# A matmul with scale and add on one core: three engines put into loops, transfers sharing semaphores, two tiles per finish

## The chip, the core and the metric

The kernel runs on one core of a Trainium2 chip. The metric is the device time of one execution in microseconds (us), less being better. The core has five engines that run programs of their own: TensorE (PE in the profile, its weight loads PEld), VectorE (DVE), ScalarE (ACT), GpSimd (POOL) and SyncE (SP). They meet at semaphores. The core's 16 DMA engines move data between memory (HBM) and the core's SBUF.

## What is computed

```python
batch, m, k, n = 16, 512, 1024, 768
def reference(x, weight, scale, add_value):
    return (scale * np.matmul(x, weight) + add_value).astype(np.float32)
```

All inputs and the output are float32: x has 16 x 512 rows of 1,024, the weight is 1,024 x 768, scale is 0.1, and add_value and the output have 16 x 512 rows of 768. That is 33.6 MB of x, 3.1 MB of weight, 25.2 MB to add and 25.2 MB to store, 87.0 MB in all.

## The kernel before

The 8,192 rows are taken as 64 tiles of 128 rows. Tiles are grouped by eight: tile s of a group is every eighth row, so that a transfer of eight tiles has one contiguous piece per partition. Each tile passes five steps:

1. SyncE issues its load of x into `xs` (16 slots of one tile) and its load of add_value into `ao` (32 slots).
2. The movers, ScalarE and GpSimd, run the same function `mover` (line 131 issues the copies). Each casts its half of x to bfloat16 into one of two buffers `va`, moving blocks of 32 partitions: eight copies per engine for a block of two or four tiles.
3. VectorE transposes two tiles at a time from `va` to `xt` (four tiles; `turn`, line 154).
4. TensorE multiplies: per tile eight chunks of the 1,024, each against 512 and 256 columns of the weight, into one of four PSUM buffers `mm` (line 194). Its program is a loop over four tiles, 16 turns.
5. VectorE computes scale times product plus add_value into the tile's slot of `ao` (`finish`, line 166), and SyncE stores it from there (line 108).

The weight lands in `ao` slots first and VectorE casts it to bfloat16 (line 142).

SyncE issues every transfer, in the order of the list `STREAM`, written by hand; its entries are (what, first tile, number of tiles), with "w" the weight, "a" add_value and "o" the store. In front of some it waits: for the moves that free the slots of x (lines 92 and 93), for the store that frees a slot of `ao` (line 103), for the finishes that a store needs (line 107). Each of the 29 transfers has a semaphore of its own, `landed`. A wait that isn't met holds all entries behind it.

The order on VectorE is written by hand too: after the finishes of a pair of tiles comes the transpose of the pair after next. The transpose of a block's first pair waits for both movers, and a finish for the landing of its add_value and for the product. ScalarE, GpSimd and VectorE have their programs written out in full, 160 copies each for the first two.

Of the kernel before, what the change touches and what calls it, by code (L numbers as in the profile page):

```python
# [7 lines left out]
P = 128  # L8
G = 8
X_SLOTS = 16  # L10
A_SLOTS = 32
CUT = 512
MM_BUFS = 4
XT_PAIRS = 2
VA_BUFS = 2

STREAM = [
# [5 lines left out]
]  # L23

MOVES = [(t, 2) for t in range(0, 8, 2)] + [(t, 4) for t in range(8, 56, 4)] + [
    (t, 2) for t in range(56, 64, 2)]


@with_exitstack
def kernel(  # L30
# [8 lines left out]
    nc = tc.nc  # L39
    bf16 = mybir.dt.bfloat16  # L40
    fp32 = mybir.dt.float32
# [25 lines left out]
    va = [const.tile([P, 4 * KC, 4, 64], bf16, name=f"va{i}") for i in range(VA_BUFS)]  # L67
    xt = const.tile([P, 2 * XT_PAIRS, KC, P], fp32, name="xt")
    mm = [psum.tile([P, 1024], fp32, name=f"mm{i}") for i in range(MM_BUFS)]

    landed = {key: tc.alloc_semaphore(f"dma{i}") for i, key in enumerate(STREAM)}
    by_act, by_pool, turned, casts, done, made = (
        tc.alloc_semaphore(name)
        for name in ("by_act", "by_pool", "turned", "casts", "done", "made"))

    def transfer(op, t):
        return next(k for k in STREAM if k[0] == op and k[1] <= t < k[1] + k[2])

    def moves_until(t):
        return 8 * sum(1 for s, _ in MOVES if s <= t)  # L80

    def sync_engine(eng):
        for key in STREAM:
            op, s, n = key
            last = s + n - 1
            if op == "w":
                k = A_SLOTS - KJ + s
                dst = ao[:, k:k + n, :].rearrange("p (c r) n -> p c (r n)", r=2)
                move = eng.dma_start(dst, w_v[:, s // 2:(s + n) // 2, :])  # L89
            elif op == "x":  # L90
                if last >= X_SLOTS:
# [3 lines left out]
                move = eng.dma_start(xs[:, k:k + n, :], rows(x_v, s, n))  # L95
            elif op == "a":
                k = s % A_SLOTS
# [6 lines left out]
                move = eng.dma_start(ao[:, k:k + n, :], rows(add_v, s, n))  # L104
            else:
                k = s % A_SLOTS
                eng.wait_ge(made, MM_BUFS + last + 1)
                move = eng.dma_start(rows(out_v, s, n), ao[:, k:k + n, :])
            move.then_inc(landed[key], 16)
        for key in STREAM:  # L110
            if key[0] == "o" and key[1] + key[2] > T - A_SLOTS:
                eng.wait_ge(landed[key], 16)

    def mover(eng, copy, parity, count):
        seen = set()
        used = [None] * VA_BUFS
        turned_after = {}
        for n, (t, size) in enumerate(MOVES):
            buf = n % VA_BUFS
            key = transfer("x", t + size - 1)  # L120
            if key not in seen:
                eng.wait_ge(landed[key], 16)
                seen.add(key)
            if used[buf] is not None:
                eng.wait_ge(turned, used[buf] + size_of[used[buf]])
            used[buf] = t
            k = t % X_SLOTS
            src = xs[:, k:k + size, :].rearrange("p i (c b k) -> p (i c) b k", b=4, k=64)
            for a in (parity, parity + 2):
                for b in range(4):  # L130
                    copy(va[buf][32 * b:32 * b + 32, 0:size * KC, a, :],  # L131
                         src[32 * a:32 * a + 32, :, b, :]).then_inc(count, 1)

    size_of = dict(MOVES)

    def vector_engine(eng):
        seen = set()

        def cast_w(s, n):
            eng.wait_ge(landed["w", s, n], 16)  # L140
            for j in range(s, s + n):
                eng.tensor_copy(w_bf[:, j, :], ao[:, A_SLOTS - KJ + j, :]).then_inc(casts, 1)  # L142

        def turn(t):
            n = next(i for i, (s, size) in enumerate(MOVES) if s <= t < s + size)
            s, size = MOVES[n]
            if t == s:
                eng.wait_ge(by_act, 8 * (n + 1))
                eng.wait_ge(by_pool, 8 * (n + 1))  # L149
            if t >= 2 * XT_PAIRS:  # L150
                eng.wait_ge(done, t - 2 * XT_PAIRS + 2)  # L151
            q = (t - s) * KC
            k = t % (2 * XT_PAIRS)
            eng.transpose(  # L154
                xt[:, k:k + 2, :, :].rearrange("p i c m -> p (i c m)"),
                va[n % VA_BUFS][:, q:q + 2 * KC, :, :].bitcast(fp32).rearrange("p c a k -> p (c a k)"),
            ).then_inc(turned, 2)

        def finish(t):
            key = transfer("a", t)  # L160
            if key not in seen:
                eng.wait_ge(landed[key], 16)
                seen.add(key)
            eng.wait_ge(done, t + 1)
            a = ao[:, t % A_SLOTS, :]
            eng.scalar_tensor_tensor(  # L166
                a, mm[t % MM_BUFS][:, 0:N], float(scale), a,
                op0=mybir.AluOpType.mult, op1=mybir.AluOpType.add).then_inc(made, 1)

        eng.sem_inc(made, MM_BUFS)  # L170
        cast_w(0, 4)
        turn(0)
        cast_w(4, 4)
        turn(2)
        for t in range(T):
            finish(t)
            if t % 2 and t + 3 < T:
                turn(t + 3)

    def tensor_engine(eng):  # L180
        eng.wait_ge(casts, 4)
        with eng.Fori(1, T + 1, 4) as i:
            for q in range(4):
                t = q
                if q % 2 == 0:
                    eng.wait_ge(turned, i + (q + 1))
                for j in range(KJ):
                    if q == 0 and j == 4:
                        eng.wait_ge(casts, KJ)
                    if j == 0:  # L190
                        eng.wait_ge(made, i + q if q else i)
                    x2 = xt[:, q, j // 2, :].bitcast(bf16).rearrange("p (m r) -> p r m", r=2)
                    for n0, n1 in ((0, CUT), (CUT, N)):
                        m = eng.matmul(  # L194
                            mm[q][:, n0:n1], x2[:, j % 2, :], w_bf[:, j, n0:n1],
                            start=(j == 0), stop=(j == KJ - 1))
                m.then_inc(done, 1)

    with tc.tile_critical(no_gpsimd_drain=True):  # L199
        sync_engine(nc.sync)  # L200
        mover(nc.scalar, nc.scalar.copy, 0, by_act)
        mover(nc.gpsimd, nc.gpsimd.tensor_copy, 1, by_pool)
        vector_engine(nc.vector)
        tensor_engine(nc.tensor)

# [34 lines left out]
```

## Time and profile before

| | |
|---|---|
| median of three runs | 211.14 us (210.84 to 212.0) |
| the profiled execution | 211.75 us, of which 210.0 us span |
| mean granted TensorE clock | 0.963 |
| busy: PE, DVE, ACT, POOL | 82%, 49%, 67%, 66% of the span |
| data moved | 87.06 MB, mean 415 GB/s over the span |
| a copy of a mover for four tiles (ACT, POOL) | 1.04 us, 1.03 us; eight in a block |
| a transpose of two tiles (DVE) | 1.24 us |
| a finish of one tile (DVE) | 0.95 us |
| 63 matmuls, about four tiles (PE) | 10.35 us |

The span is the time from the first to the last instruction of the profiled execution; the rest of its time lies outside. Times within the profile are counted from the start of the span. An engine's name with a q (SPq) is its sequencer, which issues transfers and waits. A row of the timeline gives start, duration, engine, line, operation, what is written and read, the number of instructions, and in brackets the engine's idle time before it and what ended it.

### The profile page before, as it was taken

The page shows a single profiled execution, that of the slowest core. Times are in us where ns is not written, and L with a number is a line of the kernel's source. Part 1 is how long each engine was busy: PE and PEld are TensorE (multiplying, and loading weights), DVE is VectorE, ACT ScalarE, POOL GpSimd, SP SyncE. Part 2 cuts the span into 40 slices and gives each one's busy share as a digit, 9 for nine tenths or more (in the row PEclk, how much of TensorE's full clock was granted, in tenths as well). Part 3 has the DMA queues.
Part 4 walks back from the last instruction along what each step waited for, and adds up shares of the span by engine and source line. Part 5 has one row for each costly group of instructions (what it writes and reads, how often), then busy time and mean ns, then how long its engine had stood idle before and what let it go on. Part 6 is the DMA issues. An engine that isn't in the chain of part 4 may idle for free.

```text
span 210.0 us, 2723 instructions
## 1 busy us (share of the span) xinstructions
PE 172.3 (82%) x1008; PEld 101.7 (48%) x1024; DVE 103.2 (49%) x104; ACT 140.8 (67%) x161; POOL 139.5 (66%) x164
## 2 busy tenths in 40 slices
PE   0035949928999999999999999999939999999910
PEld 0012625604655666665566665566615566665500
DVE  0158066116655565556555652766136555447410
ACT  2873980799999896944997069950999249994000
POOL 0884980799999996944998069950999239995000
PEclk9999997996999999999999999999997999999995
DMA  6999899999999999998999999999999999999991
GB/s 215 430 445 449 384 474 399 449 449 399 459 431 412 415 449 418 429 468 375 445 463 415 426 417 421 440 474 395 440 417 446 404 440 445 426 417 421 424 380 76
DMA packets 4435, 87.06 MB, mean 415 GB/s; under 512 B 464, under 2 KB 464, under 8 KB 976
## 3 DMA queue, kind: packets, MB, share of 16 engines
q1 hardware_dynamic: 4432, 87.03, 97.2%
q14 instruction: 3, 0.02, 0.0%
HBM read 61.87 MB, written 25.17 MB: 414 GB/s over the span
## 4 chain that ended last, share of the span: by engine, by line
DMA 43%; POOL 28%; PE 21%; issue 2%; SPq 1%; DVE 1%; DVEq 0%
DMA xs<-in_x_dram 43%; POOL va L131 28%; PE mm L194 21%; SPq L95 1%; DVE xt L154 1%; SPq L89 0%; DVE ao L166 0%; SPq L104 0%; DVEq L151 0%; SPq L93 0%; SPq L235 0%; DVEq L149 0%; SPq L199 0%
## 5 line engine op out<-in xcount | busy, mean ns | idle before, releaser
L194 PE MATMUL mm<-w_bf,xt 128*128 128x256 bf16 (+1 forms) x1008 | 172.3, 332 | 28.1 <-DVE xt L154 24.7
L131 POOL CAST va<-xs 32x1024 bf16<-32x1024 f32 (+1 forms) x160 | 139.3, 870 | 52.7 <-DMA xs<-in_x_dram 42.0
L131 ACT CAST va<-xs 32x1024 bf16<-32x1024 f32 (+1 forms) x160 | 139.5, 872 | 49.8 <-DMA xs<-in_x_dram 43.5
L194 PEld LDWEIGHTS mm<-w_bf,xt 128*128 128x128 bf16 x1024 | 101.7, 100 | 98.4 <-DVE xt L154 25.8
L166 DVE SCALAR_TENSOR_TENSOR ao<-mm,ao 128x768 f32<-128x768 f32 x64 | 60.3, 951 | 65.2 <-PE mm L194 52.3
L154 DVE STREAM_TRANSPOSE xt<-va 128x1024 f32<-128x1024 f32 x32 | 39.5, 1235 | 21.2 <-POOL va L131 19.9
L142 DVE CAST w_bf<-ao 128x768 bf16<-128x768 f32 x8 | 6.0, 804 | 11.8 <-DMA ao<-in_weight_dram 11.8
L131 ACT ACT_TABLE_LOAD x1 | 1.3, 1283 | 0.9 <-SPq L199 0.9
L221 POOL MEMSET const-float32-0.0<- 128x1 f32 x1 | 0.1, 97 | 0.2 <-issue 0.2
L221 POOL MEMSET const-bfloat16-1.0<- 128x1 bf16 x1 | 0.1, 100 | 0.0
L221 POOL MEMSET const-float32-1.0<- 128x1 f32 x1 | 0.1, 98 | 0.0
L221 POOL MEMSET const-uint8-127<- 128x1 uint8 x1 | 0.1, 98 | 0.0
## 6 DMA issues: line engine op xcount, KB each, us to landing
xs<-in_x_dram SPq DMA_DIRECT2D x7, 4096.0 KB, 30.4
ao<-in_add_value_dram SPq DMA_DIRECT2D x8, 3072.0 KB, 31.3
out_dram<-ao SPq DMA_DIRECT2D x7, 3072.0 KB, 35.1
ao<-in_weight_dram SPq DMA_DIRECT2D x2, 1536.0 KB, 10.8
xs<-in_x_dram SPq DMA_DIRECT2D x2, 1024.0 KB, 7.5
xs<-in_x_dram SPq DMA_DIRECT2D x1, 2048.0 KB, 17.7
out_dram<-ao SPq DMA_DIRECT2D x1, 1920.0 KB, 11.0
out_dram<-ao SPq DMA_DIRECT2D x1, 1152.0 KB, 7.0
```

The lines of the kernel that those rows point to most:

```text
L95: move = eng.dma_start(xs[:, k:k + n, :], rows(x_v, s, n))
L131: copy(va[buf][32 * b:32 * b + 32, 0:size * KC, a, :], src[32 * a:32 * a + 32, :, b, :]).then_inc(count, 1)
L142: eng.tensor_copy(w_bf[:, j, :], ao[:, A_SLOTS - KJ + j, :]).then_inc(casts, 1)
L154: eng.transpose(xt[:, k:k + 2, :, :].rearrange("p i c m -> p (i c m)"), va[n % VA_BUFS][:, q:q + 2 * KC, :, :].bitcast(fp32).rearrange("p ...
L166: eng.scalar_tensor_tensor(a, mm[t % MM_BUFS][:, 0:N], float(scale), a, op0=mybir.AluOpType.mult, op1=mybir.AluOpType.add).then_inc(made, 1)
L194: m = eng.matmul(mm[q][:, n0:n1], x2[:, j % 2, :], w_bf[:, j, n0:n1], start=(j == 0), stop=(j == KJ - 1))
L221: nc = _bacc.Bacc("TRN2", target_bir_lowering=False, num_devices=1)
```

## The change

It does these things:

- **Loops.** `mover` becomes a loop of 16 tiles a turn for ScalarE and GpSimd, with four blocks of four tiles in it (the first and last tiles went in blocks of two). VectorE's finishes and transposes become a loop of eight tiles a turn (`group`), the last eight tiles written out behind it; the slot of `ao` is computed from the loop's register. TensorE's loop keeps its four tiles.
- **Shared semaphores.** In place of one for each transfer there are three for x, two for the weight, one for all loads of add_value, two for the stores in turn. A load of add_value now waits until the one before has landed, and a store until the store before the last has. Loads of x wait for the transposes (`turned`) in place of the moves, all but that of tiles 24 to 31.
- **Two tiles per finish.** `mm` becomes one tile with four parts, and one instruction finishes two tiles. TensorE signals and waits once for two tiles. The weight is cast by two instructions in place of eight.
- **The stream.** The first four tiles of x are one transfer (two and two before), the store of tiles 24 to 31 stands behind the loads of add_value 48 to 55 and of x 56 to 63, the last two stores have six and two tiles (five and three before). Slots of `ao` are shifted by eight, so that the weight lies in the first.

```diff
 STREAM = [
-    ("x", 0, 2), ("w", 0, 4), ("x", 2, 2), ("w", 4, 4), ("x", 4, 4), ("a", 0, 8),
+    ("x", 0, 4), ("w", 0, 4), ("w", 4, 4), ("x", 4, 4), ("a", 0, 8),
     ("x", 8, 8), ("a", 8, 8), ("x", 16, 8), ("a", 16, 8), ("x", 24, 8),
     ("a", 24, 8), ("o", 0, 8), ("x", 32, 8), ("o", 8, 8), ("a", 32, 8), ("x", 40, 8),
-    ("o", 16, 8), ("a", 40, 8), ("x", 48, 8), ("o", 24, 8), ("a", 48, 8), ("x", 56, 8),
-    ("o", 32, 8), ("a", 56, 8), ("o", 40, 8), ("o", 48, 8), ("o", 56, 5), ("o", 61, 3),
+    ("o", 16, 8), ("a", 40, 8), ("x", 48, 8), ("a", 48, 8), ("x", 56, 8), ("o", 24, 8),
+    ("o", 32, 8), ("a", 56, 8), ("o", 40, 8), ("o", 48, 8), ("o", 56, 6), ("o", 62, 2),
 ]
...
+    TURNED = MOVE * VA_BUFS
+    MADE = TURNED + 2 + MM_BUFS - 2
+
+    def slot(t):
+        return (t + G) % A_SLOTS
...
                 if last >= X_SLOTS:
-                    eng.wait_ge(by_act, moves_until(last - X_SLOTS))
-                    eng.wait_ge(by_pool, moves_until(last - X_SLOTS))
-                k = s % X_SLOTS
+                    free = last + 1 - X_SLOTS
+                    if s == 24:
+                        eng.wait_ge(by_act, 8 * free // MOVE)
+                        eng.wait_ge(by_pool, 8 * free // MOVE)
+                    else:
+                        eng.wait_ge(turned, TURNED + free)
...
-                if s < A_SLOTS <= last + KJ:
+                if loads:
+                    eng.wait_ge(a_sem, 16 * len(loads))
+                if slot(s) == 0:
                     eng.wait_ge(casts, KJ)
                 if s >= A_SLOTS:
-                    for key2 in STREAM:
-                        if key2[0] == "o" and key2[1] < last + 1 - A_SLOTS and key2[1] + key2[2] > s - A_SLOTS:
-                            eng.wait_ge(landed[key2], 16)
+                    i = stores.index((s - A_SLOTS, n))
+                    eng.wait_ge(o_sem[i % 2], 16 * (i // 2 + 1))
...
-                eng.wait_ge(made, MM_BUFS + last + 1)
+                i = len(stores)
+                if i > 1:
+                    eng.wait_ge(o_sem[i % 2], 16 * (i // 2))
+                eng.wait_ge(made, MADE + last + 1)
...
+    def mover(eng, copy, parity, count, go=None):
+        with eng.Fori(16, 16 * (T // X_SLOTS) + 1, 16) as i:
+            for q in range(X_SLOTS // MOVE):
+                if q < 3:
+                    eng.wait_ge((x_lo, x_mid, x_hi)[q], i)
+                eng.wait_ge(turned, i + (4 * q - 12) if q < 3 else i)
...
+        def finish(pair, at, products):
+            eng.wait_ge(done, products)
+            a = ao_g[:, at, 2 * pair:2 * pair + 2, :]
+            q = 2 * (pair % 2)
             eng.scalar_tensor_tensor(
-                a, mm[t % MM_BUFS][:, 0:N], float(scale), a,
-                op0=mybir.AluOpType.mult, op1=mybir.AluOpType.add).then_inc(made, 1)
+                a, mm[:, q:q + 2, 0:N], float(scale), a,
+                op0=mybir.AluOpType.mult, op1=mybir.AluOpType.add).then_inc(made, 2)
+
+        def group(i, at, last):
+            eng.wait_ge(a_sem, i)
+            for p in range(4):
+                finish(p, at, i + (4 * p - 12) if p < 3 else i)
+                if p < 2 or not last:
+                    turn(1 if p < 2 else 0, p % 2, i + 8 if p == 2 else i)
...
+        with eng.Fori(16, 2 * T, 16) as i:
+            group(i, bass.ds((i // 16) % (A_SLOTS // G), 1), False)
+        s = slot(T - G) // G
+        group(2 * T, slice(s, s + 1), True)
```

In the changed kernel the movers' copies stand on line 137, the casts of the weight on 145, the transposes on 152, the finishes on 161 and the matmuls on 193; SyncE's loads of x are on 100, of add_value on 110, the stores on 118.

More of the change, by code (lines that the diff above doesn't have):

```diff
@@ L13 @@
 MM_BUFS = 4
-XT_PAIRS = 2
+XT_TILES = 4
 VA_BUFS = 2
+MOVE = 4
+AHEAD = 4
 STREAM = [
[1 row of a table removed]
[1 row of a table added]
     ("x", 8, 8), ("a", 8, 8), ("x", 16, 8), ("a", 16, 8), ("x", 24, 8),
     ("a", 24, 8), ("o", 0, 8), ("x", 32, 8), ("o", 8, 8), ("a", 32, 8), ("x", 40, 8),
[2 rows of a table removed]
-]
-MOVES = [(t, 2) for t in range(0, 8, 2)] + [(t, 4) for t in range(8, 56, 4)] + [
-    (t, 2) for t in range(56, 64, 2)]
[2 rows of a table added]
+]
 @with_exitstack
@@ L66 @@
     w_bf = const.tile([P, KJ, N], bf16, name="w_bf")
[L67 to L72, printed above, removed]
-        tc.alloc_semaphore(name)
-        for name in ("by_act", "by_pool", "turned", "casts", "done", "made"))
@@ L76, in transfer @@
[L76 to L80, printed above, removed]
+    va = [const.tile([P, MOVE * KC, 4, 64], bf16, name=f"va{i}") for i in range(VA_BUFS)]
+    xt = const.tile([P, XT_TILES, KC, P], fp32, name="xt")
+    mm = psum.tile([P, MM_BUFS, 1024], fp32, name="mm")
+    w_sem = [tc.alloc_semaphore(f"w{i}") for i in range(2)]
+    x_lo, x_mid, x_hi, a_sem = (tc.alloc_semaphore(n) for n in ("x_lo", "x_mid", "x_hi", "a"))
@@ L82, in sync_engine @@
+    o_sem = [tc.alloc_semaphore(f"o{i}") for i in range(2)]
+    by_act, by_pool, pool_go, turned, casts, done, made = (
+        tc.alloc_semaphore(name)
+        for name in ("by_act", "by_pool", "pool_go", "turned", "casts", "done", "made"))
+    TURNED = MOVE * VA_BUFS
+    MADE = TURNED + 2 + MM_BUFS - 2
+    def slot(t):
+        return (t + G) % A_SLOTS
     def sync_engine(eng):
-        for key in STREAM:
-            op, s, n = key
+        loads, stores = [], []
+        for op, s, n in STREAM:
@@ L85, in sync_engine @@
             last = s + n - 1
             if op == "w":
-                k = A_SLOTS - KJ + s
-                dst = ao[:, k:k + n, :].rearrange("p (c r) n -> p c (r n)", r=2)
-                move = eng.dma_start(dst, w_v[:, s // 2:(s + n) // 2, :])
+                dst = ao[:, s:s + n, :].rearrange("p (c r) n -> p c (r n)", r=2)
+                move, sem = eng.dma_start(dst, w_v[:, s // 2:(s + n) // 2, :]), w_sem[s // 4]
             elif op == "x":
+                k = s % X_SLOTS
                 if last >= X_SLOTS:
-                    eng.wait_ge(by_act, moves_until(last - X_SLOTS))
-                    eng.wait_ge(by_pool, moves_until(last - X_SLOTS))
@@ L94, in sync_engine @@
-                k = s % X_SLOTS
+                    free = last + 1 - X_SLOTS
[4 more added lines that the diff above has]
+                        eng.wait_ge(turned, TURNED + free)
+                    if s == X_SLOTS:
+                        eng.sem_inc(x_mid, 16 * (T // X_SLOTS - 1))
                 move = eng.dma_start(xs[:, k:k + n, :], rows(x_v, s, n))
+                sem = x_mid if s == 4 else x_hi if k else x_lo
@@ L96, in sync_engine @@
             elif op == "a":
-                k = s % A_SLOTS
-                if s < A_SLOTS <= last + KJ:
+                if loads:
+                    eng.wait_ge(a_sem, 16 * len(loads))
+                if slot(s) == 0:
                     eng.wait_ge(casts, KJ)
                 if s >= A_SLOTS:
-                    for key2 in STREAM:
-                        if key2[0] == "o" and key2[1] < last + 1 - A_SLOTS and key2[1] + key2[2] > s - A_SLOTS:
-                            eng.wait_ge(landed[key2], 16)
@@ L104, in sync_engine @@
-                move = eng.dma_start(ao[:, k:k + n, :], rows(add_v, s, n))
-            else:
-                k = s % A_SLOTS
-                eng.wait_ge(made, MM_BUFS + last + 1)
[L108 to L132, printed above, removed]
@@ L134 @@
-    size_of = dict(MOVES)
+                    i = stores.index((s - A_SLOTS, n))
+                    eng.wait_ge(o_sem[i % 2], 16 * (i // 2 + 1))
+                move = eng.dma_start(ao[:, slot(s):slot(s) + n, :], rows(add_v, s, n))
+                sem = a_sem
+                loads.append((s, n))
+            else:
+                i = len(stores)
+                if i > 1:
+                    eng.wait_ge(o_sem[i % 2], 16 * (i // 2))
+                eng.wait_ge(made, MADE + last + 1)
+                move = eng.dma_start(rows(out_v, s, n), ao[:, slot(s):slot(s) + n, :])
+                sem = o_sem[i % 2]
+                stores.append((s, n))
@@ new lines, in sync_engine @@
+            move.then_inc(sem, 16)
+        for i in (len(stores) - 2, len(stores) - 1):
+            eng.wait_ge(o_sem[i % 2], 16 * (i // 2 + 1))
+    def mover(eng, copy, parity, count, go=None):
[4 more added lines that the diff above has]
+                eng.wait_ge(turned, i + (4 * q - 12) if q < 3 else i)
+                if go is not None:
+                    eng.sem_inc(go, 1)
+                k = MOVE * q
+                src = xs[:, k:k + MOVE, :].rearrange("p i (c b k) -> p (i c) b k", b=4, k=64)
+                for a in (parity, parity + 2):
+                    for b in range(4):
+                        copy(va[q % VA_BUFS][32 * b:32 * b + 32, :, a, :],
+                             src[32 * a:32 * a + 32, :, b, :]).then_inc(count, 1)
@@ L136, in vector_engine @@
     def vector_engine(eng):
-        seen = set()
+        ao_g = ao.rearrange("p (g t) n -> p g t n", t=G)
         def cast_w(s, n):
[L140 to L153, printed above, removed]
+            eng.wait_ge(w_sem[s // 4], 16)
+            eng.tensor_copy(w_bf[:, s:s + n, :], ao[:, s:s + n, :]).then_inc(casts, n)
@@ L154, in turn @@
+        def turn(move, half, moves=None):
+            if half == 0:
+                eng.wait_ge(by_act, moves)
+                eng.wait_ge(by_pool, moves)
+            q = 2 * half * KC
             eng.transpose(
-                xt[:, k:k + 2, :, :].rearrange("p i c m -> p (i c m)"),
-                va[n % VA_BUFS][:, q:q + 2 * KC, :, :].bitcast(fp32).rearrange("p c a k -> p (c a k)"),
+                xt[:, 2 * half:2 * half + 2, :, :].rearrange("p i c m -> p (i c m)"),
+                va[move % VA_BUFS][:, q:q + 2 * KC, :, :].bitcast(fp32).rearrange("p c a k -> p (c a k)"),
@@ L157, in turn @@
             ).then_inc(turned, 2)
[L159 to L166, printed above, removed]
-                a, mm[t % MM_BUFS][:, 0:N], float(scale), a,
-                op0=mybir.AluOpType.mult, op1=mybir.AluOpType.add).then_inc(made, 1)
-        eng.sem_inc(made, MM_BUFS)
+        def finish(pair, at, products):
+            eng.wait_ge(done, products)
+            a = ao_g[:, at, 2 * pair:2 * pair + 2, :]
+            q = 2 * (pair % 2)
+            eng.scalar_tensor_tensor(
+                a, mm[:, q:q + 2, 0:N], float(scale), a,
+                op0=mybir.AluOpType.mult, op1=mybir.AluOpType.add).then_inc(made, 2)
@@ L171, in vector_engine @@
+        def group(i, at, last):
[4 more added lines that the diff above has]
+                    turn(1 if p < 2 else 0, p % 2, i + 8 if p == 2 else i)
         cast_w(0, 4)
-        turn(0)
         cast_w(4, 4)
[L174 to L178, printed above, removed]
-    def tensor_engine(eng):
[L181 to L184, printed above, removed]
+        turn(0, 0, 8)
@@ L185, in tensor_engine @@
+        turn(0, 1)
+        with eng.Fori(16, 2 * T, 16) as i:
+            group(i, bass.ds((i // 16) % (A_SLOTS // G), 1), False)
+        s = slot(T - G) // G
+        group(2 * T, slice(s, s + 1), True)
+    def tensor_engine(eng):
+        eng.sem_inc(turned, TURNED)
+        eng.sem_inc(made, MADE)
+        eng.wait_ge(casts, KJ)
+        with eng.Fori(TURNED + 2, TURNED + 2 + T, XT_TILES) as i:
+            for q in range(XT_TILES):
                 if q % 2 == 0:
-                    eng.wait_ge(turned, i + (q + 1))
+                    eng.wait_ge(turned, i + q if q else i)
+                    eng.wait_ge(made, i + q if q else i)
@@ L187, in tensor_engine @@
                 for j in range(KJ):
[L188 to L191, printed above, removed]
                     x2 = xt[:, q, j // 2, :].bitcast(bf16).rearrange("p (m r) -> p r m", r=2)
@@ L194, in tensor_engine @@
                         m = eng.matmul(
-                            mm[q][:, n0:n1], x2[:, j % 2, :], w_bf[:, j, n0:n1],
+                            mm[:, q, n0:n1], x2[:, j % 2, :], w_bf[:, j, n0:n1],
                             start=(j == 0), stop=(j == KJ - 1))
-                m.then_inc(done, 1)
+                if q % 2:
+                    m.then_inc(done, 4)
     with tc.tile_critical(no_gpsimd_drain=True):
@@ L201 @@
         mover(nc.scalar, nc.scalar.copy, 0, by_act)
-        mover(nc.gpsimd, nc.gpsimd.tensor_copy, 1, by_pool)
+        mover(nc.gpsimd, nc.gpsimd.tensor_copy, 1, by_pool, pool_go)
         vector_engine(nc.vector)
```

## The prediction

> **What bounds the kernel now.** I read the page first: slices, DMA queues, chain of waits. The columns of the first row are 40 slices of 5.25 us.
>
> ```profile
> DMA  6999899999999999998999999999999999999991
> ...
> q1 hardware_dynamic: 4432, 87.03, 97.2%
> q14 instruction: 3, 0.02, 0.0%
> ```
>
> The transfers fill the 16 DMA engines from the first slice to the last but one, while no compute engine passes 82%. The view by windows says it by stage (its last three columns: granted clock, DMA share, GB/s):
>
> ```profile
> 55.00:98.00 43.00, 42.79 (x263) 25.92 (x266) 25.93 (x26) 33.79 (x33) 33.89 (x34) 1.00 1.00 426
> 98.00:147.00 49.00, 48.74 (x298) 29.49 (x302) 29.04 (x29) 32.96 (x33) 32.69 (x33) 1.00 1.01 432
> 147.00:187.00 40.00, 36.50 (x214) 21.49 (x216) 17.81 (x18) 31.84 (x41) 30.91 (x40) 0.96 1.00 427
> ```
>
> The queue is never dry between 2 and 187 us. All transfers stand in one queue, in order, so the end is bytes over rate, plus whatever makes the queue dry, plus whatever slows single DMA engines. The chain of waits (43% on loads of x) walks through the same queue by its landings.
>
> Then the landing events of the trace: each transfer has 16, one per DMA engine. After its transfer, when the first, the twelfth and the last engine landed:
>
> ```
> x 16-23     54.39   54.51   54.73
> add 16-23   61.69   61.86   62.55
> add 24-31   78.75   79.00   79.97
> x 32-39     95.75   96.02   97.36
> x 48-55    144.24  144.57  146.77
> add 56-63  183.03  183.34  186.56
> last store 205.42  205.60  208.40
> ```
>
> Twelve engines stay together; two pairs fall behind in steps and at the end lag by 1.6 to 1.9 and by 2.8 us. The last pair sets the end: 208.40, then 1.58 us of closing barriers to the span's 209.98, then 1.77 us outside the span to the profiled execution's 211.75. That execution lies 0.61 above the median of 211.14, so I subtract on the profiled execution and put the result on the median.
>
> What starts the lag? The three instruction packets (8,192 bytes, about 0.31 us each) run at 54.91, 54.93 and 80.27. On their DMA engines the next packets of 24,576 bytes take 1.36, 1.35 and 1.27 us, against 0.91 for nearly all others. ScalarE, GpSimd and VectorE had then executed 56, 60 and 62 of their 177, 186 and 171 recorded instructions. So I take it that each fetched the rest of its unrolled program there. The other slow packets (near 77, 95, 119, 144, 182 and 183.5 us) have no instruction packet ahead of them.
>
> **Loops on three engines.** With all three programs shorter by more than half, I expect none of the three packets in the span. Worth: the fetches at 54.9 hit the pair that sets the end. Between x 16-23 and add 16-23 its lag behind the twelfth engine grew from 0.22 to 0.69, so 0.47; by packets it is 0.31 + 0.44 = 0.75. I take 0.6. The third packet hits a pair that ends 0.9 earlier, so it is worth nothing at the end.
>
> Turning costs, in before: TensorE's loop already turns 16 times, and 63 matmuls fill 10.35 us of its 10.4 us per turn, so a turn costs under 0.1, and no instruction packet lies at any of its turns. Of the movers' three new turns two lie where they wait for x anyway (5.8 us before x 32-39, 7.5 before x 48-55), the third, before x 16-23, costs its 0.1; VectorE's six lie behind 2 us of slack, worked out below. Nothing on the path. [...]
>
> **Two tiles per finish.** Before, per tile and per pair:
>
> ```profile
> 80.92 0.96 DVE L166 SCALAR_TENSOR_TENSOR ao<-mm,ao 128x768 f32<-128x768 f32 x1 [1.64 <-PE mm L194]
> 81.79 1.24 DVE L154 STREAM_TRANSPOSE xt<-va 128x1024 f32<-128x1024 f32 x1
> ```
>
> The first tile of a pair was finished under the second tile's matmuls; now both are finished after the pair. 2 x 0.96 less the overlap of 0.09 gives 1.83, plus 1.24: 3.0 us from TensorE's end of a pair to the transposed pair after next. TensorE works 2 x 2.6 = 5.2 us on the pair between, so 2.1 us cover it, also the address arithmetic that the finish gets for its slot in the loop (no row; TensorE's register steps hide in under 0.1 a turn, and the longest idle that the groups put down to issue is 0.28, on its weight loads; I take 0.1, between 0 and 0.28). The eight weight casts become two (8 x 0.80 against about the same 6.4), in the first 19 us, ahead of add 0-7 at 28.0.
>
> **Waits on the queue of SyncE.** Everything behind a wait there waits too, so I ask for each transfer whether it is issued before the twelve leading engines end the one ahead, less 0.9 us (the last store was issued at 201.44 and its packets began at 202.3). All adds now share one semaphore, so each waits until the add before has landed:
>
> - add 8-15 at 28.0 (x 8-15 ends 37.4), add 16-23 at 45.0 (54.4), add 24-31 at 62.5 (71.4), add 40-47 at 112 (o 16-23 ends 127.6), add 48-55 at 136.8 (144.2). Covers of 6.5 us or more.
> - x now waits for transposes instead of moves. Transposes of before plus the 0.9 us that the double finish is later: x 16 at 35 (add 8-15 ends 44.7); x 40 at 105 against 110.3; x 48 at 125.5 against 134.5; x 56 at 146.3 against 151.7 (add 48-55, now in the slot of store 24-31). Covers 4 us or more.
> - x 32 is the narrow one. It was issued at
>
> ```profile
> 72.80 0.33 SPq L95 DMA_DIRECT2D xs<-in_x_dram  x1
> ```
>
> and now waits for the transpose of tiles 22 and 23, the 81.79 row above: TensorE's pair ends at 80.9, finish 1.8, transpose 1.24, address 0.1, so 84.1. The store ahead ends at 86.3 on the leading engines: cover 86.3 - 0.9 - 84.1 = 1.3 us. It was 12.6. The pair that sets the end is 0.9 behind there, 0.3 without the fetch, so only lateness beyond 1.6 us costs.
>
> The move of store 24-31 puts it behind add 48-55 and x 56-63, which land 7.3 us (one 3 MB slot) earlier. Add 56-63 waits for that store at about 171, with store 32-39 (7.3 us) queued behind it as cover. No byte is added: zero. x 48 stays in its place, and the compute tail hangs on it:
>
> ```profile
> 146.82 14.16 POOL L131 CAST va<-xs 32x1024 bf16<-32x1024 f32 x13 [7.05 <-DMA xs<-in_x_dram]
> ...
> 155.72 1.25 DVE L154 STREAM_TRANSPOSE xt<-va 128x1024 f32<-128x1024 f32 x1 [6.25 <-POOL va L131]
> ...
> 157.02 3.38 PE L194 MATMUL mm<-w_bf,xt 128*128 128x512 bf16 x10 [3.34 <-DVE xt L154]
> ```
>
> From there TensorE runs through to 200.43.
>
> **The last stores.** Before: 200.46 + 0.96, store of three tiles at 201.44, on the leading engines landed at 205.5. Now the pair ends at 200.46 + 1.83 = 202.3, but the store is two tiles, 0.91 us shorter to move (393 KB at 431 GB/s): 205.5 again. Six tiles go out at 197.2 in place of five at 194.7; the leading engines idle 0.3 to 0.6 there, the lagging ones (busy to 201.09) do not. Zero.
>
> First loads: x in one piece of four tiles starts TensorE at about 20 instead of 13.7, but x 8-15 (37.7) and its moves (46.5) restart TensorE at 48 in both. Zero.
>
> Sum: 211.75 - 0.6 = 211.15 on the profiled execution, 211.14 - 0.6 = 210.5 on the median.
>
> **Rivals.**
> 1. The whole lag goes. Slow packets may follow from the first: once a pair is out of step, it reads elsewhere than the others. For it: the steps after 55 keep hitting the same four engines. Against: near 77 us about half of the engines were slowed, and no instruction packet is near. Then the last landing is 205.5 and the time 205.5 + 1.58 + 1.77 = 208.9.
> 2. Slower: the queue runs dry ahead of x 32. Decides: lateness of that transpose beyond 1.6 us, if the finish of two tiles with an address from registers takes about twice my 1.9. Price: each us beyond is a us; 3.5 us late gives 210.5 + 1.9 = 212.4. Against: VectorE is at 49%, and two plain finishes in a row take 1.78 in this trace.
> 3. The loops do not spare the fetches, or other slow packets are drawn instead: 211.1, no change.
>
> **How the numbers follow.** Forecast 0.55, rival 1 0.22, rival 2 0.10, rival 3 0.13. The measurement tells about 0.5% (1.06 us) from no change: faster means under 210.1, slower over 212.2. Faster: rival 1's 0.22 and 0.08 of the forecast, where the pair loses more than 1 us = 0.30; slower 0.10; the rest, 0.60, is within. The range takes in rival 1 (with 0.1 for clearing fewer semaphores at the close, a row of 0.27, 208.8) and stops short of rival 2 at 212.0, which also holds a run with as many slow packets as the profiled one and no saving. The likeliest case alone: 210.1 to 211.1.
>
> **What would show it.** Right: no instruction packet in the span; landings of add 16-23 together within 0.3; the last landing at 207 to 208; the window 55 to 187 still at DMA share 1.00; x 32 issued near 84; the finish near 1.8. Wrong: a slice under 9 near 86 us (rival 2), instruction packets at loop turns, or a last landing near 205.5 (rival 1).

## The result, and the profile after

The changed kernel is slower: a median of 212.53 us (22 runs, 211.05 to 213.72) against 211.12 (22 runs, 210.64 to 212.0) for the kernel before, a ratio of 1.0059 with a 95% interval of 1.0040 to 1.0077. I had forecast 210.5, and 212.0 as the upper end. The runs also scatter over 2.7 us in place of 1.4. The profiled execution took 211.79 us with a span of 209.7, so it is 0.7 under the median; a second profile, in the third group of experiments, took 212.56.

The page first: slices of the DMA engines, and the queue row.

```profile
DMA  6999999999999999999999999999999999999886
...
q1 hardware_dynamic: 4288, 87.03, 97.8%
```

The row of instruction packets is gone, as forecast. But the two slices before the last fell from 9 to 8: there DMA engines wait. The last one rose from 1 to 6, since most engines now end later (the twelfth of the 16 landed the last store at 208.21 in place of 205.60). The windows of the stages (last three columns: granted clock, DMA share, GB/s):

```profile
55.00:98.00 43.00, 43.00 (x266) 25.87 (x265) 24.63 (x17) 34.54 (x33) 33.50 (x33) 1.00 1.00 415
98.00:147.00 49.00, 48.33 (x299) 28.87 (x297) 27.82 (x20) 34.65 (x33) 33.09 (x32) 1.00 1.00 433
147.00:187.00 40.00, 35.80 (x207) 20.74 (x206) 17.50 (x13) 34.65 (x33) 33.10 (x32) 0.91 1.00 432
```

The engines are as busy as before, and still the first stage moves 415 GB/s in place of 426. Busy is not fast here. Narrowed to the 13 us in which x 32-39 is loaded, before and then after:

```profile
84.00:97.00 13.00, 12.95 (x82) 7.83 (x81) 7.09 (x8) 7.40 (x8) 7.37 (x8) 1.00 0.99 423
```

```profile
84.00:97.00 13.00, 13.00 (x82) 7.84 (x80) 6.18 (x5) 8.21 (x8) 8.27 (x8) 1.00 0.99 381
```

The timeline of SyncE's queue has this load at the time that I forecast (84.1):

```profile
83.86 0.33 SPq L100 DMA_DIRECT2D xs<-in_x_dram  x1
```

In the trace 34 of its 128 packets of 32,768 bytes take 1.4 to 2.4 us, at two places, near 86 to 88 (its first) and near 93 to 97 (its last), on nearly all engines, against 1.22 otherwise. It landed 12.25 us after the store ahead of it; in the kernel before, x 16-23 and x 24-31, loads of the same size, landed 9.71 and 9.72 us after the transfer ahead. Spread between the first and the last of the 16 engines' landings, in us, in profiled executions:

```
                         add 16-23  add 24-31  x 32-39  add 48-55  add 56-63  store 48-55
before                      0.86       1.22      1.61      2.56       3.54       3.56
after                       0.39       0.33      2.41      2.38       2.63       2.67
after, second profile       0.45       0.41      2.27      2.28       3.15       3.19
```

The timeline of the tail (the first row is the table load of ScalarE):

```profile
147.42 1.28 ACT L137 ACT_TABLE_LOAD   x1 [7.18 <-DMA xs<-in_x_dram]
...
157.32 1.25 DVE L152 STREAM_TRANSPOSE xt<-va 128x1024 f32<-128x1024 f32 x1 [6.20 <-ACT va L137]
...
158.62 44.13 PE L193 MATMUL mm<-w_bf,xt 128*128 128x512 bf16 x256 [4.20 <-DVE xt L152]
...
202.85 1.76 DVE L161 SCALAR_TENSOR_TENSOR ao<-mm,ao 128x1536 f32<-128x1536 f32 x1 [3.44 <-PE mm L193]
```

x 48-55 landed at 147.33. Before, its move ended 8.9 us after the landing; now a table load of 1.28 us, begun 0.09 after the landing, stands ahead of ScalarE's copies, and it takes 10.0. TensorE starts 1.6 later and then needs 44.1 us for the 16 tiles in place of 43.4. Its clock was granted at half for 6.8 us from 156.61 on, so for the first 4.8 us of this work; before, for 3.4 us from 156.94 on, of which 3.3 fell on the work. The 16 tiles took 0.72 us longer with 1.5 us more of it at half. The last store is issued at 204.69 in place of 201.44. The sum: landing 0.56, table and its wake-up 1.04, clock 0.72, double finish 0.93: 3.25.

Two bounds now lie close together. The leading engines run dry and land the last store at 208.07, 3.4 us after its issue. The most lagging engine never runs dry: its last three landings are at 200.94, 206.41 and 208.25, so 5.47 and 1.84 us for the stores of six and two tiles, 7.31 together; for the eight tiles of store 48-55 the last landing had moved on by 7.23 (193.71 to 200.94). In the second profile they are at 201.72, 207.19 and 209.03, with the leading engines at 208.35. So in both the lagging engines are the later bound, by 0.2 and 0.7 us.

### The profile page after: what moved, and what is told of

Same layout as the page of the kernel before. It is cut to its first block, busy times and chain, and to the rows that moved or that the text cites. A ratio compares the mean times of both kernels' runs of the same rounds, so it can differ in the third digit from the quotient of the medians.

```text
span 209.7 us, 2739 instructions
## 1 busy us (share of the span) xinstructions
PE 173.4 (83%) x1024; PEld 101.9 (49%) x1024; DVE 97.7 (47%) x66; ACT 138.6 (66%) x132; POOL 135.4 (65%) x132
## 4 chain that ended last, share of the span: by engine, by line
PE 63%; DMA 14%; POOL 9%; ACT 4%; DVE 4%; issue 3%; DVEq 0%; POOLq 0%; SPq 0%; ACTq 0%
PE mm L193 63%; DMA xs<-in_x_dram 14%; POOL va L137 9%; ACT va L137 4%; DVE xt L152 3%; DVE ao L161 1%; ACT L137 1%; DVEq L150 0%; DVEq L161 0%; POOLq L132 0%; POOLq L130 0%; ACTq L130 0%; SPq L235 0%; DVEq L158 0%; SPq L199 0%
## 5 line engine op out<-in xcount | busy, mean ns | idle before, releaser
L193 PE MATMUL mm<-w_bf,xt 128*128 128x512 bf16 (+1 forms) x1024 | 173.4, 334 | 29.3 <-DVE xt L152 29.3
L137 POOL CAST va<-xs 32x1024 bf16<-32x1024 f32 x128 | 135.2, 1056 | 47.8 <-DMA xs<-in_x_dram 29.0
L137 ACT CAST va<-xs 32x1024 bf16<-32x1024 f32 x128 | 133.5, 1043 | 22.4 <-DVE xt L152 10.9
L161 DVE SCALAR_TENSOR_TENSOR ao<-mm,ao 128x1536 f32 (+1 forms) x32 | 56.1, 1754 | 77.1 <-PE mm L193 77.1
L137 ACT ACT_TABLE_LOAD x4 | 5.1, 1283 | 22.1 <-DMA xs<-in_x_dram 22.1
L145 DVE CAST w_bf<-ao 128x3072 bf16<-128x3072 f32 x2 | 4.5, 2238 | 13.6 <-DMA ao<-in_weight_dram 13.6
## 6 DMA issues: line engine op xcount, KB each, us to landing
ao<-in_weight_dram SPq DMA_DIRECT2D x2, 1536.0 KB, 12.3
```

The costliest lines, as they stand in the source:

```text
L137: copy(va[q % VA_BUFS][32 * b:32 * b + 32, :, a, :], src[32 * a:32 * a + 32, :, b, :]).then_inc(count, 1)
L145: eng.tensor_copy(w_bf[:, s:s + n, :], ao[:, s:s + n, :]).then_inc(casts, n)
L161: eng.scalar_tensor_tensor(a, mm[:, q:q + 2, 0:N], float(scale), a, op0=mybir.AluOpType.mult, op1=mybir.AluOpType.add).then_inc(made, 2)
L193: m = eng.matmul(mm[:, q, n0:n1], x2[:, j % 2, :], w_bf[:, j, n0:n1], start=(j == 0), stop=(j == KJ - 1))
```

## The experiments

Two theories went into them. T1: the compute chain from the landing of x 48-55 sets the end, with the table load and the double finish in it. T2: DMA engines that fell behind at the late load of x 32-39 set the end.

All are compared by their ratio to the kernel before on the same chip; 12 runs each where nothing else is said. Three of them (the table load ahead, both edits, and single finishes with both edits) also begin 0.23 us later, since a memset for the one-element copy precedes the first load (issued at 1.17 in place of 0.94).

| Experiment | median us | ratio (95% interval) |
|---|---|---|
| e1 table load ahead of the wait | 212.02 | 1.0041 (1.0018 to 1.0064) |
| e2 x 32-39 waits for moves | 211.43 | 1.0012 (0.9996 to 1.0029) |
| e3 both | 211.22 | 1.0011 (0.9995 to 1.0027) |
| e4 both, single finishes at the end | 211.33 | 1.0007 (0.9991 to 1.0023) |
| b1 kernel before, x 32-39 late | 211.93 | 1.0049 (1.0035 to 1.0063), 11 runs |
| u1 as e2, ScalarE written out | 211.02 | 1.0005 (0.9993 to 1.0017) |
| u2 as e2, ScalarE and GpSimd written out | 210.80 | 0.9988 (0.9978 to 0.9998) |
| s1 as e2, store 24-31 in its old place | 211.82 | 1.0060 (1.0029 to 1.0092), 8 runs |
| f1 changed kernel, single finishes at the end | 212.14 | 1.0047 (1.0032 to 1.0062) |
| d1 changed kernel, x 32-39 issued at 79 | 211.49 | 1.0011 (0.9998 to 1.0025) |
| b2 kernel before, store 24-31 later | 210.90 | 0.9994 (0.9977 to 1.0011) |
| t1 as u2, x 32-39 ahead of store 0-7 | 210.78 | 0.9973 (0.9959 to 0.9988) |
| t2 as e2, GpSimd written out | 211.00 | 0.9991 (0.9977 to 1.0005) |
| t3 as e2, again | 211.41 | 1.0005 (0.9990 to 1.0020) |
| t4 as u2, again | 210.81 | 0.9976 (0.9961 to 0.9990) |

### First group: is it the late load or the compute chain?

e1, the table load:

```diff
+            if go is None:
+                copy(warm[0:1, 0:1], warm[0:1, 1:2])
             for q in range(X_SLOTS // MOVE):
```

> A one-element copy at the head of ScalarE's loop draws the table load ahead of the wait for x. Theory T1 (the chain from the landing of x 48-55 through TensorE sets the end, and the table load stands in it): the move of tiles 48-51 ends about 1.0 us sooner after the landing (10.0 to 9.0 us), and the time falls by 1.0 to 1.7 us from the 212.5 of the changed kernel, to 210.8 to 211.5. Theory T2 (the end is set by DMA engines that fell behind at x 32-39, which is issued late): no change, 212.3 to 212.7.

ScalarE's timeline in e1 shows the load seven us ahead of the landing that it stood behind:

```profile
138.67 1.28 ACT L129 ACT_TABLE_LOAD   x1
```

The transpose of tiles 48 and 49 began 9.1 us after the landing in place of 10.0, as T1 said. The median fell by 0.5, to a ratio of 1.0041; with the 0.23 of the later begin it is about 0.7. That lies between the two theories, and the interval overlaps that of the changed kernel, so the table load may be a part of the loss but is not shown to be one by this run. The scatter stayed (210.5 to 213.2).

The profiled execution of e1 is the fastest of its runs (210.54), and there the load of x 32-39 went out 1.1 us sooner:

```profile
82.75 0.33 SPq L101 DMA_DIRECT2D xs<-in_x_dram  x1
```

The table load didn't do this: the one at 54.89 in the changed kernel stands at 55.08 in e1. But TensorE's clock had no stretch at half near 48 us there, against 3.4 us from 47.39 on in the changed kernel, and the finish of its first pair began at 53.93 in place of 55.04. With 1.1 us more ahead, 10 packets of x 32-39 were slow in place of 34, and the spread there was 1.08.

e2, the late load:

```diff
-                    if s == 24:
+                    if s in (24, 32):
```

> The load of x 32-39 waits for the moves of tiles 16 to 23 again, as it did before, instead of for the transposes; all else as in the changed kernel. T2: x 32-39 is issued near 73 instead of 83.9, its packets are no longer slow near 86 and 94, the spread of the engines' landings after it falls from 2.4 to about 0.4 us, and the time falls by 2 us to about 210.5. T1: x 48-55 lands 0.5 to 2 us sooner and the end moves with it by that, to 210.5 to 212, and the scatter of runs (211.1 to 213.7) shrinks; the last store still lands 3.5 to 4 us after the last finish.

```profile
73.27 0.33 SPq L100 DMA_DIRECT2D xs<-in_x_dram  x1
```

```profile
84.00:97.00 13.00, 12.95 (x81) 7.84 (x81) 6.05 (x5) 9.11 (x9) 8.91 (x9) 1.00 0.99 423
```

423 GB/s again, no slow packet left near 86 or 94, a spread of 0.46 at x 32-39, and the time is 1.1 lower with runs from 211.18 to 212.06. The packets and the spread are as T2 said, the gain is half of its 2 us. This one line is worth most of the slowdown, and the scatter is down to 0.9 us.

e3 and e4, both edits, and then the last eight tiles finished one by one (`done` rises by 2 a tile):

> Both edits: table load ahead of the wait, x 32-39 waiting for moves. T1: the savings add up, 1.0 to 1.7 and 0.5 to 2 off 212.5: 209.5 to 211. T2: as x 32-39 alone, 210.5.

> As the run with both edits, and the last eight tiles are finished one by one, TensorE signalling each tile. T1: the last finish takes 0.96 in place of 1.76 us, so the last store is issued 0.8 to 0.9 us sooner after TensorE's end: 0.8 below the run with both edits, as long as the DMA engines are not the bound (floor near 208.9). T2: no change against it.

e3 lies 0.2 under e2 by medians and nothing by ratios (1.0011 and 1.0012), within the intervals; its later begin hides a further 0.2 us at most. T1's sum, 209.5 to 211, isn't reached. e4 gains nothing on e3. Once the late load is mended, lagging DMA engines set the end by a wide margin: in e3 the leading ones landed the last store at 205.11, the last one at 207.89. A shorter last finish can't help there.

### Second group: each part by itself

b1, the late load in the kernel before:

```diff
+                    if s == 32:
+                        eng.wait_ge(turned, last + 1 - X_SLOTS)
+                    else:
                         eng.wait_ge(by_act, moves_until(last - X_SLOTS))
                         eng.wait_ge(by_pool, moves_until(last - X_SLOTS))
```

> The kernel before, with one edit: the load of x 32-39 waits for the transpose of tiles 22 and 23 in place of the moves, so it is issued near 83 instead of 72.8. Theory T2 (a load that reaches the queue only some 3 us before its turn has slow packets on all engines): spread of landings at x 32-39 up from 0.5 to 1 or more, over 2 in some executions, the runs scatter over 2 us or more, and the median rises by 0.5 to 1.5 from 211.1. Theory T1 (only the compute chain of the changed kernel matters, with its table load and double finish): no change, 211.0 to 211.3.

```profile
84.11 0.33 SPq L98 DMA_DIRECT2D xs<-in_x_dram  x1
```

```profile
84.00:97.00 13.00, 12.95 (x81) 7.82 (x81) 7.18 (x8) 8.34 (x8) 8.28 (x8) 1.00 0.98 367
```

One moved wait, in a kernel without any loop or double finish added: 367 GB/s in these 13 us, a spread of 2.89 at x 32-39, and 1.0 us slower, as T2 said, with runs over 1.5 us in place of the 2 that it expected. This shows the late load as a cause of its own. The store behind it went out late with it (84.48), but still 12.3 us before x 32-39 first landed. Why the packets of a late load are slow is not shown. It costs less at the end than where it arises: x 32-39 landed 2.3 later than before, but the spread then grew by 0.3 up to store 48-55 (from 2.89 to 3.22), against 2.0 in the kernel before.

u1 and u2, the loops undone for ScalarE, and for GpSimd too (`for i in range(16, 65, 16)` in place of `Fori`):

> The changed kernel with x 32-39 waiting for moves, and ScalarE's mover written out in full: one table load in place of four, and one instruction packet should be back in the span. If fetches feed the lag as the prediction had it: 0.3 to 0.6 above 211.4, less 0.2 for the table. If the lag comes from elsewhere: 0 to 0.4 below 211.4, since the table load no longer stands ahead of the last chain.

> As the run before, and GpSimd's mover written out too, so two instruction packets. If fetches feed the lag: 211.8 or more. If not: the same as with ScalarE alone, 211.0 to 211.4.

The instruction packets are back, one and then two, near 76 us. No cost of them shows at the end: the median of u1 lies 0.4 under e2 and that of u2, 210.80, 0.6 under it, below both ranges expected. That is across two chips; the fourth group has the comparison on one. The saving that I had put on the loops isn't there, and the loops cost instead.

s1, the store of tiles 24 to 31 back in its old place:

```diff
-    ("o", 16, 8), ("a", 40, 8), ("x", 48, 8), ("a", 48, 8), ("x", 56, 8), ("o", 24, 8),
+    ("o", 16, 8), ("a", 40, 8), ("x", 48, 8), ("o", 24, 8), ("a", 48, 8), ("x", 56, 8),
```

> The changed kernel with x 32-39 waiting for moves, and the store of tiles 24 to 31 back behind the load of x 48-55, where it stood before. The prediction put the move of this store at zero: 211.2 to 211.6. If the moved store costs something by the change from loads to stores: lower by 0.3 or more.

Slower than e2, which neither expectation had: by 0.4 in the medians, 0.5 when each is taken against the kernel before on its chip, and 1.0 by the ratios, which three of the eight runs at 212.6 to 214.1 pull up. x 56-63 lands at 171.1, and with blocks of four tiles its first pair waits for a whole block:

```profile
180.14 1.25 DVE L152 STREAM_TRANSPOSE xt<-va 128x1024 f32<-128x1024 f32 x1 [3.59 <-POOL va L137]
...
181.44 10.79 PE L193 MATMUL mm<-w_bf,xt 128*128 128x512 bf16 x64 [1.60 <-DVE xt L152]
```

TensorE stands for 1.6 us, and its last matmul ends at 202.4 (199.0 in e2). The rest of these 3.4 us comes earlier: tile 48 starts 0.6 later, and there TensorE's clock was at half for 3.4 us, in e2 not at all. By this trace the move of the store pays for the loss of the two-tile blocks; no run with smaller blocks shows it.

### Third group: how late is late?

> The changed kernel, with the last eight tiles finished one by one (TensorE signals each tile); x 32-39 late and table load as they are. Theory T1 (in the changed kernel the end is set by the compute chain, the DMA engines wait for the last stores): 0.8 below 212.5, 211.5 to 211.9. Theory T2 (the DMA engines' lag after x 32-39 sets the end): no change, 212.3 to 212.7.

f1 came 0.4 under the changed kernel, half of what T1 says, and its interval overlaps that of the changed kernel: the compute chain isn't the only bound, and how much of one is not settled by this run. In its profile the leading engines end at 207.68, the last at 208.87.

d1 waits for the moves and for the transpose of tiles 20 and 21 (`turned, TURNED + free - 2`):

> The changed kernel, with x 32-39 waiting for the moves and for the transpose of tiles 20 and 21, so it is issued near 78.7: a cover of 6.6 us ahead of its turn in place of 1.6 (waiting for moves alone gave 12). If the slow packets come of reaching the queue with 2 us of work left: all of the 1.1 is gone, 211.2 to 211.7. If any later issue costs in proportion: about half is left, 211.9 to 212.1.

```profile
79.28 0.33 SPq L104 DMA_DIRECT2D xs<-in_x_dram  x1
```

```profile
84.00:97.00 13.00, 13.00 (x83) 7.82 (x81) 6.09 (x5) 9.03 (x9) 8.82 (x9) 1.00 0.98 419
```

Issued 7.1 us before the store ahead first lands (86.38), the load is as good as at 13 (e2): 211.49, a spread of 0.53. At 2.0 to 2.4 (b1, the changed kernel) it is slow. Other traces narrow the gap: x 56-63 in e2 and in this run, issued 4.8 us ahead by the same count, kept its spread (1.14 and 0.95), and e1's 3.8 us for x 32-39 cost a part. So 4.8 us (there behind another load) cost nothing that shows, 3.8 a part and 2.0 to 2.4 the full 1.0 to 1.1 us: not in proportion to the time lost. In e1, with no stretch at half near 48 us, the issue came 1.1 us sooner, so some of the scatter of the changed kernel may come from TensorE's clock there; one execution doesn't prove it.

> The kernel before, with the store of tiles 24 to 31 moved behind the loads of add 48-55 and x 56-63, nothing else. The prediction put the move at zero: 210.7 to 211.2. If the earlier x 56-63 helps the compute chain here as it does with blocks of four tiles (moving it back cost 0.4 there): 210.5 to 210.8.

b2: no change that can be measured in the kernel before, as predicted for the move alone.

> The changed kernel again, for a second look at its profile. The first was 0.7 under the median. T1 and T2 both: x 32-39 is issued near 84 with slow packets near 86 and 94. T1: with x 48-55 landing at time t, the last store is issued near t + 57.4 and lands 3.6 later. T2: the last store lands 6 or more after its issue.

The second profiled execution took 212.56. x 48-55 landed at 147.47 and the last store was issued at 204.95, as expected; it landed 4.1 later, between what the two theories said.

### Fourth group: what the loops cost, and whence the lag

> The changed kernel with x 32-39 waiting for moves, both movers in loops, again, beside the others of this call. Loops cost something beyond the late load: 0.3 to 0.6 above the kernel with both movers written out. They cost nothing and the earlier difference was the chip: within 0.2 of it.

> The changed kernel with x 32-39 waiting for moves, GpSimd's mover written out, ScalarE's still in the loop with its four table loads. If GpSimd's loop costs by itself: 0.2 below the kernel with both loops. If all of the 0.4 to 0.6 is ScalarE's table load: no change against both loops.

> Both movers written out, x 32-39 waiting for moves, again. As before: 0.1 under the kernel before (ratio 0.998 to 1.000). If fetches cost 0.6 as predicted, it would be 0.6 above the kernel with both loops; the first run spoke against that.

Side by side on one chip: both movers in loops 211.41, GpSimd written out 211.00, both written out 210.81. By ratios, which take every run in, ScalarE's loop alone is worth 0.0007 and 0.0015 (e2 to u1, t2 to t4), GpSimd's alone 0.0014 and 0.0017 (t3 to t2, u1 to u2), both 0.0024 and 0.0029 (e2 to u2, t3 to t4): 0.15 to 0.3, 0.3 to 0.4 and 0.5 to 0.6 us. Each has an interval of about 0.3 us on either side, so the sum of both stands out, and GpSimd's part comes out alike twice. TensorE's rows of t3 and t2:

```profile
156.93 1.46 PE L193 MATMUL mm<-w_bf,xt 128*128 128x512 bf16 x4 [4.55 <-DVE xt L152]
```

```profile
156.52 1.69 PE L200 MATMUL mm<-w_bf,xt 128*128 128x512 bf16 x9 [2.60 <-DVE xt L159]
```

TensorE's idle time ahead of tile 48, and how long its clock was granted at half from there, by the trace's clock records:

```
                     idle us   half clock us   last matmul ends
d1                     2.45        3.4              199.9
t2                     2.60        0                198.7
e2                     2.64        0                199.0
e1                     3.26        3.4              199.4
before                 3.34        3.4              200.4
u1                     3.68        3.4              199.7
after, second profile  4.18        6.8              203.0
after                  4.20        6.8              202.7
f1                     4.22        6.8              203.2
t3                     4.55        6.8              201.6
```

In these ten profiles the time at half was 0, 3.4 or 6.8 us, and the more of it fell on the work, the longer the work took, by about half of the difference: 3.3, 4.8 and 5.8 us of it in before, after and t3, 43.4, 44.1 and 44.6 us for the 16 tiles. The idle time is not lateness alone: in t3 TensorE started 0.41 later than in t2, but it had also ended tile 47 1.5 us sooner (152.38 and 153.92), having had no stretch at half near 48 us. In t3 the leading engines run dry (206.88 at the end) though x 32-39 is early; the last one still lands 1.3 later, at 208.16. t2 has the table load and yet a short idle time, so the path from GpSimd's loop to the time isn't shown: in e2 and t2 lagging DMA engines set the end, and why they lag less without that loop stays open.

> Both movers written out, x 32-39 waiting for moves, and the load of x 32-39 put ahead of the store of tiles 0 to 7, so that loads give way to stores four times in place of five. If the lag that sets the end grows at those changes: the step near 77 us or that near 95 is missing, and the time falls 0.3 to 0.6 below the same kernel with five. If the lag comes at random or with bytes: no change, within 0.2.

t1 took the same time as t4 (210.78 and 210.81). So one change from loads to stores less took nothing off the lag that sets the end; what makes it stays open too. t1 and t4 are faster than both kernels, by 0.27% and 0.24% against the kernel before; which part of the change gives this is not shown.

## Why the prediction was wrong

- **The cover of x 32-39** is the step that failed. I found the place, the issue time (84.1, measured 83.86) and the narrowness, and priced it by the wrong question: whether the queue runs dry. It did not: the DMA share stayed at 0.99, and against e2 the first engine lost 0.7 us and the last 2.7 on slow packets. By my count the load wasn't late at all, yet the late issue alone costs 1.0 us (b1), and undoing it gains 1.1 (e2). In place of "only lateness beyond 1.6 us costs" I should have asked how short a cover the trace of before shows to be harmless. Once the queue is full, the shortest for a load there is 6.4 us (x 24-31, issued at 55.30 while the load ahead first lands at 61.69); below that the price was unknown and should have gone into the range. Rival 2 had the place and the sign at 0.10, with a mechanism that did not occur.
- **0.6 off for the instruction fetches.** The packets went as forecast, and add 16-23 landed within 0.39 us (0.86 before, 0.3 forecast). The error was to take what the fetch added at 55 us off the end as well. The lag grew again without it: e2, with no packet, ends with a spread of 2.88 at store 48-55, t4, with two, with 3.48, and t4 is the faster by its runs. No run shows anything of the 0.6 at the end, as rival 3 had it; where the loops were undone the packets come at 76 to 78 us, so the ones at 55 were not tested by themselves.
- **Loops cost nothing on the path.** The turns themselves show no cost in the profile after: at the third and fourth the movers began 0.09 (ScalarE) and 0.23 to 0.24 us (GpSimd) after x had landed, and at x 40-47, within a turn, 0.10 and 0.23 (written out, in the kernel before, 0.02 to 0.03 and 0.05 to 0.06). But each of ScalarE's four turns begins with a table load (at 8.38, 54.89, 98.92 and 147.42), which I had not priced although the kernel before has its row (1,283 ns, once). In the changed program it stands behind the wait for x, so of the four the last one is on the compute tail (1.04 us there, with its wake-up). What it is worth at the end by itself isn't settled (e1, e3); both loops together cost 0.5 to 0.6 us (u2, t4). The groups of the profile after have it as

```profile
L137 ACT ACT_TABLE_LOAD x4 | 5.1, 1283 | 22.1 <-DMA xs<-in_x_dram 22.1
```

- **TensorE's clock** was not in the sum. The idle time grew from 3.34 to 4.20, and half speed lasted 6.8 us in place of 3.4, worth 0.72 on the compute tail. What starts a stretch at half is not shown: d1 had one of 3.4 us after idling 2.45 us, t2 none after 2.60.
- **The last stores at zero, the moved store at zero.** Right while lagging engines set the end (e3 against e4, b2). In the changed kernel the compute chain had come within 0.2 of them (208.07 and 208.25): the store of six tiles went out at 199.49, not at 197.2 as forecast, after the table load, the clock and the later landing. There the finish may count in part (f1, intervals overlap); with blocks of four tiles the moved store is worth 0.4 to 1.0 (s1).
- **The waits on the shared semaphore of add_value** were right: every load of add_value was issued within 1.4 us of the forecast, and from the second on each landed 7.2 to 7.4 us after the transfer ahead (first engine's landings; 6.9 to 7.3 in the kernel before). The finish of two tiles took 1.76 (1.83 forecast).

## What to carry to other kernels

In this kernel it was not enough to issue a load just before the DMA queue was dry: x 32-39 issued 2.0 to 2.4 us before the store ahead first landed cost a full us (b1, the changed kernel), 7.1 us ahead nothing (d1), at a busy share of 0.98 to 0.99 in all three. So ask for each transfer how far ahead of its turn it is issued, and read GB/s in a narrow window (367, 381 and 419 here), not the share alone. Before putting ScalarE's work into a loop, look in the built order at where the table load stands; ahead of the wait it took 0.9 us off ScalarE's chain here, of which the time showed no sure gain. A disturbance taken out early in a long queue is not worth its size at the end until an experiment shows that the end moves.

## What the runs showed of the hardware that was not expected

- A load that joined the queue 2.0 to 2.4 us before the store ahead of it first landed had packets of up to 2.8 us in place of 1.22, not only at its head but also at its end 8 us later, on nearly all of the 16 engines (both profiles of after, b1, f1). At 3.8 us ten were slow (e1, 34 to 41 in the others), from 7.1 us up at most six, of up to 1.95 (d1 two, e2 none, b2 six). Why isn't shown. A store issued 2.8 us ahead (tiles 56 to 60, before) had none.
- The engines' spread grew less after the late loads: from x 32-39 to store 48-55 by 0.3 to 0.9 us in b1 and the two profiles of after, where it was 2.3 to 2.9 at x 32-39, by 1.0 in e1 (1.08 there), and by 2.0 and 2.4 in the kernel before and e2 (1.61 and 0.46). Why isn't shown.
- Ahead of tile 48, TensorE's clock after idling 2.45 to 3.7 us was at half for none or one stretch of 3.4 us, after 4.2 us or more for two. The length of the idle time does not decide it: ahead of tile 8 (near 48 us) one stretch followed 4.22 us in d1 and 4.87 in the kernel before, two followed 3.09 in e4, and none 3.51 in e1.
